# A two-layer recurrent trunk: the keys and values of layer 2 transposed in 32x32 blocks by VectorE and rearranged through DRAM instead of by TensorE, and queries and gates through one Silu

## The chip, the cores and the metric

One core of a Trainium2 chip runs the whole kernel in one launch. The metric is the time on the device in microseconds (us), the median of three runs. The profile shows one more execution, recorded by the hardware profiler. Its engines are TensorE (PE; its loads of the stationary operand are listed as PEld), VectorE (DVE), ScalarE (ACT), GpSimd (POOL) and SyncE (SP), whose queue issues nearly all of the DMAs.

## The reference

One inference step of two layers, for 1024 prompt tokens and 8 samples of 4 tokens each, width 1024. Layer 1 is a gated linear recurrence with a short convolution (RG-LRU). Layer 2, where most of the change lies, is HGRN2: eight heads with 128 key and 128 value channels, a matrix state per head, and an output gate.

```python
def _hgrn_layer(x, g_norm, w_in, lb, o_gain, w_out, S0):
    xn = _rmsnorm(x, g_norm)
    u = (xn @ w_in).astype(jnp.float32)
    q, f, iv, gate = jnp.split(u, 4, axis=-1)
    q = jax.nn.silu(q).reshape(Bsz, T, H_B, DK_B)
    log_g = jnp.logaddexp(jnp.log(lbh), jnp.log1p(-lbh) + jax.nn.log_sigmoid(f.reshape(Bsz, T, H_B, DK_B)))
    k = -jnp.expm1(log_g)
    v = iv.reshape(Bsz, T, H_B, DV_B)
    o, S_T = _hgrn2_chunked(q, k, v, log_g, S0)
    o = o * lax.rsqrt(jnp.mean(o * o, axis=-1, keepdims=True) + EPS) * o_gain.reshape(H_B, DV_B)
    y = (o.reshape(Bsz, T, INNER_B) * jax.nn.silu(gate)).astype(x.dtype)
    return x + y @ w_out, S_T
```

`_hgrn2_chunked` computes, chunk by chunk, causal attention within the chunk under the decays, plus the queries times the state that earlier chunks left; and it carries the state on by the sum over the chunk's tokens of key times value. For that sum the tokens must lie on the contracted axis.

## The kernel before, in words

All activations are kept transposed: 128 channels on the partitions, 1056 tokens (1024 of the prompt, 32 of the samples) along the row. Products are made in single-pass float32 from split operands: x = xh + xl and w = wh + wl, three matmuls a 128x128 block (`mm3`, lines 243 to 245). In layer 1 and for layer 2's first two heads a product has 352 tokens at a time; from the third head on a seven-product scheme (`seven`) makes two projections of a head together from products of 264 tokens.

**The order of the work.** Every operation is entered into a `Flow` with an engine, an estimated cost, the keys that it reads and writes, and a priority. `Flow.plan` lists the operations by a model of the engines, eight times over with due times from a backward pass, and the best list is emitted as it is: each engine then executes its own list in order. In layer 2 the PE operations are chained (`pe`, `main=True`), so PE keeps the order in which the program enters them; what the planner chooses is the order on DVE, ACT, POOL and SP. DMAs go on SP's queue and an instruction there that waits holds up those behind it.

**A head in layer 2.** The projections of a head give queries (row `arow`), the forget gate, from which decays `Gs` and keys (`brow`) are made, output gate (`SG[h]`) and values (`VT`). Between the projection's products of the next heads stand four bursts of small work for the attention:

- `burst1(h)`: decay levels 0 and 1 of head h; keys and values of head h-1 turned so that tokens lie on the partitions (`keys_`, `values`).
- `burst2(h)`: levels 2 and 4 of head h; `states(h-1)`: eight matmuls of `kt` (stationary) with `vt` (moving), one for each chunk of 128 tokens, and the running state in `SA`; the samples' states (`advance`).
- `burst3(h)`: `outs(h-1)`: attention times `vt` plus queries times state, squares and norms into `on`; levels 8 and 16 of head h.
- `burst4(h)`: `gated(h-1)` turns `on` back by PE and multiplies it by the gate; levels 32 and 64 of head h, and the first half of head h's values turned (`values(h, (0,))`).

The last multiply of a head's keys before they are turned is the one of level 64, in `scale` (line 1036), entered in `burst4`. The turning itself is `transposed` (lines 1154 to 1169): four transposes of 128x128 on PE into one PSUM bank, copied by ACT into `kt` or `vt`; it is used four times a head, twice for each of the two. `kt` and `on` are one buffer. `vt` lies in `rows[5]`.

Silu is made of Tanh: z times (1 + tanh(z/2)), twice the Silu. ACT takes the Tanh, DVE multiplies (`scalar_tensor_tensor`), in `first1` (lines 716 and 717) for the first head's queries, in `item` (1009 and 1018) for the rest of heads 0 and 1, and in `settle` (1517 and 1518) from head 2 on. The factor 2 of the queries is made good by 4 times EPS in the norm, that of the gate by `hog`, half the output gain.

Products go into three PSUM banks in turn (`mm`), small work into five (`hg`), while `seven` runs; DVE adds the products together (`plus`, line 1503). Weights come by DMA into five buffers in turn, are added and subtracted by DVE (line 1440), cast by ACT (line 1430), and their rest is taken by POOL (line 325).

## Time and profile before

| | |
|---|---|
| median of 3 runs | 1060.99 us (1060.94 to 1062.35) |
| span of the profiled execution, first to last instruction | 1059.4 us |
| TensorE clock granted, mean | 0.996 |
| layer 1 ends, layer 2 begins, about | 508 us |
| DMA traffic | 103.07 MB, mean 97 GB/s |

The span is that of another execution than the three runs, and it leaves out what lies ahead of the first instruction and behind the last. Busy times are sums over an engine's instructions. Those of PE's matmuls overlap, since they are pipelined: what one costs is seen in the distance from its start to the next one's.

The rows that the next part quotes are of these kinds. A wait: who waited, for whom, us in all, how often, longest. A group of instructions: line, engine, operation, out<-in by the program's names, shapes and count, then busy us and mean ns, then idle us ahead of it. One line's instructions: durations as min/median/max in ns, start of the first and the last. A timeline row: start in us, us that the row covers, and how many instructions are merged in it. A DMA row: count, KB of each, median us from issue to landing.

### The profile page before, as it was taken

The numbers are of one execution on the slowest core, as the hardware profiler recorded it, in microseconds if no ns is written. First come the engines' busy times: TensorE is split into PE (matmuls) and PEld (weight loads), VectorE is DVE, ScalarE is ACT, GpSimd is POOL, SyncE is SP. The second block draws the span as 40 slices with busy tenths as digits, with TensorE's granted clock in tenths as the row PEclk, the third lists the DMA queues.
The fourth block names the chain that finished last, engine by engine and source line by source line (L and its number), as shares of the span: only waits on it lengthen the run. The fifth ranks groups of instructions, "written<-read, shape, count | busy, mean of one in ns | idle before, by whom it ended". The sixth has DMA issues, their size and how long they took to land.

```text
span 1059.4 us, 25677 instructions
## 1 busy us (share of the span) xinstructions
PE 1050.1 (99%) x9964; PEld 1021.2 (96%) x9964; DVE 842.2 (79%) x1671; ACT 590.9 (56%) x1339; POOL 540.0 (51%) x601
## 2 busy tenths in 40 slices
PE   9999999999999999999999999999999999999997
PEld 9999999999999999999999999999999999999986
DVE  7999996888888689265799988988979797994536
ACT  6568656877775875233354474646464555652324
POOL 3425343444544366555667555555545565551544
PEclk9999999999999999999999999999999999999998
DMA  8201112123842595340211121212121221355204
GB/s 297 68 27 45 54 51 74 57 60 100 255 145 63 177 294 162 127 136 28 71 44 38 45 101 44 92 45 92 35 91 54 72 70 66 117 177 167 84 3 164
DMA packets 70121, 103.07 MB, mean 97 GB/s; under 512 B 9200, under 2 KB 50160, under 8 KB 70000
## 3 DMA queue, kind: packets, MB, share of 16 engines
q1 hardware_dynamic: 67696, 98.67, 29.2%
q10 hardware_dynamic: 2304, 2.77, 0.8%
q8 instruction: 78, 1.28, 0.5%
q14 instruction: 43, 0.35, 0.1%
HBM read 71.05 MB, written 25.49 MB: 91 GB/s over the span
## 4 chain that ended last, share of the span: by engine, by line
PE 89%; DVE 6%; DMA 2%; POOL 1%; issue 1%; ACT 0%; ACTq 0%; POOLq 0%; DVEq 0%; SPq 0%
PE mm L243 24%; PE mm L244 24%; PE mm L245 24%; PE hg L569 1%; PE hg L1054 1%; PE hg L1163 1%; DVE R L1370 1%; PE hg L1273 1%; DMA wraw<-in_w_dram 1%; PE hg L1219 1%; PE hg L243 1%; PE hg L244 1%; PE hg L245 1%; PE hg L1275 1%; DVE tmp L1370 1%
## 5 line engine op out<-in xcount | busy, mean ns | idle before, releaser
L243 PE MATMUL mm<-xh,whi 128*128 128x352 f32 (+1 forms) x1143 | 358.6, 314 | 0.0
L245 PE MATMUL mm<-xh,wlo 128*128 128x352 f32 (+1 forms) x1143 | 353.2, 309 | 0.0
L244 PE MATMUL mm<-xl,whi 128*128 128x352 f32 (+1 forms) x1143 | 353.1, 309 | 0.0
L325 POOL TENSOR_TENSOR wlo<-wraw,whi 128x256 fp32r<-128x256 f32 (+3 forms) x184 | 203.3, 1122 | 178.6 <-ACT whi L380 81.2
L244 PEld LDWEIGHTS mm<-xl,whi 128*128 128x128 f32 x1143 | 215.1, 188 | 1.5
L243 PEld LDWEIGHTS mm<-xh,whi 128*128 128x128 f32 x1143 | 214.7, 188 | 1.5
L245 PEld LDWEIGHTS mm<-xh,wlo 128*128 128x128 f32 x1143 | 214.8, 188 | 0.0
L501 DVE SCALAR_TENSOR_TENSOR k<-xb,prm_sb,k 128x352 f32<-128x352 f32 (+2 forms) x144 | 90.1, 637 | 10.9 <-ACT k L498 7.7
L243 PE MATMUL mm<-t,whi 128*128 128x264 f32 (+1 forms) x306 | 89.3, 292 | 0.0
L244 PE MATMUL mm<-t,whi 128*128 128x264 f32 (+1 forms) x306 | 87.7, 287 | 0.0
L245 PE MATMUL mm<-t,wlo 128*128 128x264 f32 (+1 forms) x306 | 87.4, 286 | 0.0
L1503 DVE TENSOR_TENSOR k<-mm,k 128x264 f32<-128x264 f32 x144 | 60.2, 426 | 20.5 <-PE mm L245 17.4
L325 POOL TENSOR_TENSOR wlo<-R,whi 128x256 fp32r<-128x256 f32 x64 | 60.1, 959 | 24.7 <-ACT whi L1430 24.7
L584 POOL TENSOR_TENSOR k<-X 128x352 f32<-128x352 f32 x36 | 44.9, 1257 | 47.8 <-DVE R L585 38.6
L380 ACT CAST whi<-wraw 128x512 fp32r<-128x512 f32 (+2 forms) x83 | 46.1, 574 | 30.1 <-PE mm L244 16.1
L243 PEld LDWEIGHTS mm<-t,whi 128*128 128x128 f32 x306 | 57.6, 188 | 0.2
L245 PEld LDWEIGHTS mm<-t,wlo 128*128 128x128 f32 x306 | 57.7, 188 | 0.0
L244 PEld LDWEIGHTS mm<-t,whi 128*128 128x128 f32 x306 | 57.6, 188 | 0.0
L1430 ACT CAST whi<-wraw 128x512 fp32r<-128x512 f32 x52 | 32.1, 618 | 36.3 <-PE mm L245 16.8
L243 PE MATMUL mm<-yh,whi 128*128 128x352 f32 x153 | 49.9, 326 | 0.0
L245 PE MATMUL mm<-yh,wlo 128*128 128x352 f32 x153 | 49.4, 323 | 0.0
L244 PE MATMUL mm<-yl,whi 128*128 128x352 f32 x153 | 49.4, 323 | 0.0
(481 smaller groups left out, 2634.3 us busy)
## 6 DMA issues: line engine op xcount, KB each, us to landing
wraw<-in_w_dram SPq DMA_DIRECT2D x90, 256.0 KB, 2.7
wraw<-in_wo_dram SPq DMA_DIRECT2D x34, 192.0 KB, 2.5
si<-in_s_in_dram SPq DMA_DIRECT2D x8, 512.0 KB, 3.8
out_ss_out_dram<-si SPq DMA_DIRECT2D x8, 512.0 KB, 2.6
R<-in_w_dram SPq DMA_DIRECT2D x15, 256.0 KB, 2.5
sg<-x1b SPq DMA_DIRECT2D x21, 176.0 KB, 2.9
x<-sg SPq DMA_DIRECT2D x21, 176.0 KB, 1.8
R<-td SPq DMA_DIRECT2D x72, 44.0 KB, 2.0
```

The source lines that it names most:

```text
L243: T.matmul(out, wh, xh, start=first, stop=False)
L244: T.matmul(out, wh, xl, start=False, stop=False)
L245: T.matmul(out, wl, xh, start=False, stop=last)
L325: emit = lambda: e.tensor_tensor(b, x, a.bitcast(F32), op=ALU.subtract)
L380: act(m, lambda hi=hi, raw=raw, m=m: S.copy(hi[:, :m], raw[:, :m]), rk, (hk,), prio)
L501: dve(u, lambda src=src, dst=dst, sh=sh, k=k: V.scalar_tensor_tensor(dst, sh(src, k), pc("cw", 12 * k + m), dst, op0=ALU.mult, op1=ALU.add ...
L569: fl.add("PE", 0.62, lambda ps=ps, i=i, c=c: T.matmul(ps[:96, :CH], gs[:, i, :], ST[:96, chunk(c)], start=True, stop=True), (("gs",), *((" ...
L584: pool(CH, lambda x=x, a=a, b=b: G.tensor_tensor(x, a.bitcast(F32), b.bitcast(F32), op=ALU.add), (ak, bk), (xk,), 3)
L1054: T.matmul(ps[32 * j:32 * j + 32, n * w:n * w + w], B[:, o:o + 32], q(slice(o, o + 32)), start=True, stop=True, tile_position=(0, 32 * j))
L1370: dve(n, lambda: V.tensor_tensor(o, a, b, op=op), r, (w,), prio, True)
L1430: act(512, lambda: S.copy(hi, raw), (rk,), (hk,), 2)
L1503: dve(QT, lambda: V.tensor_tensor(o[0], z[0], u[0], op=ALU.add), (z[1], u[1]), (o[1],), 0)
```

## The change

Two things are changed.

*Turning keys and values.* `transposed` goes. `turned` takes its place, entered at the end of `burst4(h)`, once for the values (source `VT`) and once for the keys (source `brow(h, 0)`). One DVE instruction transposes each 32x32 block of a 128x1024 row within itself; a DMA writes the result, 512 KB, to DRAM (two buffers in turn for each of `vt` and `kt`); four DMAs read it back, one for each 32 partitions, 128 KB each in runs of 256 floats, so that blocks land on the partitions of their tokens. `vt` then holds a chunk's 128 value channels as four runs of 32 neighbouring floats; `kt` holds a chunk's 128 key channels eight floats apart, so that one step runs through all of them. The keys of the planner are four for each of the two, one for each 32 partitions, and all four are waited for.

*Silu.* ACT's Silu activation writes queries and gates at once; DVE's multiply goes, `hog` gives way to the output gain, 4 * EPS to EPS. The forget gate keeps its Tanh. Layer 1's own gates keep Tanh and multiply.

```diff
             if i == 0:
                 o, ok = pairs[1][:, 0, q], [("R", 1, 0, c)]
-                act(CH, lambda: S.activation(o, ps[:, :CH], AF.Tanh, scale=0.5), (pk,), ok, 0)
-                dve(CH, lambda: V.scalar_tensor_tensor(o, o, 1.0, ps[:, :CH], op0=ALU.add, op1=ALU.mult), (pk, *ok), ok, 0)
+                act(CH, lambda: S.activation(o, ps[:, :CH], AF.Silu), (pk,), ok, 0)
...
-        kt = fixed("kt", [128, 8, 128], F32, p1)
-        on = kt
+        on = fixed("kt", [128, 8, 128], F32, p1)
+        kflat = on.rearrange("p n d -> p (n d)")
...
-        vt = rows[5][:, :1024].rearrange("p (n d) -> p n d", n=8)
+        vflat = rows[5][:, :1024]
+        vt, kt = vflat.rearrange("p (a n j) -> p n a j", a=4, n=8), kflat.rearrange("p (a j n) -> p n (a j)", a=4, n=8)
+        VK, KK = ([(o, i) for i in range(4)] for o in ("vt", "kt"))
+        turn = {(o, i): nc.dram_tensor(f"{o}_{i}", (128, 1024), F32, kind="Internal").ap() for o in ("vt", "kt") for i in range(2)}
...
-                    dve(CH, lambda: V.scalar_tensor_tensor(o[:, q], t, 1.0, ps, op0=ALU.add, op1=ALU.mult), (pk, tk), k, 0)
+                    act(CH, lambda: S.activation(o[:, q], ps, AF.Silu), (pk,), k, 0)
...
-        def transposed(row, rk, dst, key, parts):
...
-                        T.transpose(ps[:, n * 128:(n + 1) * 128], row[:, a:a + 128], ident)
...
-                act(512, lambda i=i, ps=ps: S.copy(dst[:, 4 * i:4 * i + 4, :].rearrange("p n d -> p (n d)"), ps), (pk,), ((key, i),), 2)
+        def turned(h, row, rk, dst, key, keys):
+
+            d = turn[key, h % 2]
+            blocks = dst.rearrange("p (b n j) -> p b n j" if key == "vt" else "p (b j n) -> p b n j", b=4, n=8)
+            dve(1024, lambda: V.transpose(blocks, row[:, :1024].rearrange("p (n b i) -> p b n i", n=8, b=4)), rk, keys, 3)
+            dma(d, dst, keys, ((key, "d", h % 2),), 3, 512)
+            back = d.rearrange("(a i) (b m) -> b i a m", a=4, b=4)
+            for b in range(4):
+                dma(dst[32 * b:32 * b + 32].rearrange("p (a m) -> p a m", a=4), back[b], ((key, "d", h % 2),), (keys[b],), 3, 128)
...
-                        T.matmul(ps[:, n * 128:(n + 1) * 128], kt[:, 4 * i + n, :], vt[:, 4 * i + n, :], start=True, stop=True)
-
-                pe(0.94, emit, (("kt", i), ("vt", i)), (pk,))
+                        T.matmul(ps[:, n * 128:(n + 1) * 128], kt[:, 4 * i + n], vt[:, 4 * i + n], start=True, stop=True)
+
+                pe(0.94, emit, (*KK, *VK), (pk,))
...
-            run(together([*([gated(h - 1, *s)] if h else []), *([levels3264(h, *s), values(h, (0,))] if h < H else [])]))
+            run(together([*([gated(h - 1, *s)] if h else []), *([levels3264(h, *s)] if h < H else [])]))
+            if h < H:
+                turned(h, VT, [("VT", c) for c in range(4)], vflat, "vt", VK)
+                turned(h, *brow(h, 0), kflat, "kt", KK)
...
-                act(QT, lambda: S.activation(o[:, q], c, AF.Tanh, scale=0.5), (ck,), k, 0)
-                dve(QT, lambda: V.scalar_tensor_tensor(o[:, q], o[:, q], 1.0, c, op0=ALU.add, op1=ALU.mult), (ck, *k), k, 0, own)
+                act(QT, lambda: S.activation(o[:, q], c, AF.Silu), (ck,), k, 0)
```

57 lines of the change are left out of this document (20 added, 37 removed).

## The prediction

> **What bounds the kernel now.** I read the page's first part, the chain that ended last, TensorE's own waits, and then stretches of the span. First the page:
>
> ```profile
> span 1059.4 us, 25677 instructions
> PE 1050.1 (99%) x9964; PEld 1021.2 (96%) x9964; DVE 842.2 (79%) x1671; ACT 590.9 (56%) x1339; POOL 540.0 (51%) x601
> PE 89%; DVE 6%; DMA 2%; POOL 1%; issue 1%; ACT 0%; ACTq 0%; POOLq 0%; DVEq 0%; SPq 0%
> ```
>
> TensorE (PE) is busy for 1050.1 of 1059.4 us and holds 89% of the chain. A busy PE could still hide stalls, so I look at whom it waited for:
>
> ```profile
> PE hg L730 <- DVE ones L255: 1.0, 1, 1.0
> PE hg L1108 <- DVE a L1036: 0.5, 1, 0.5
> PE mm L243 <- DVE sg L529: 0.5, 1, 0.5
> PE mm L1683 <- DVE sg L1673: 0.4, 1, 0.4
> PE hg L1054 <- DVE R L1066: 0.4, 1, 0.4
> ```
>
> All its waits come to 2.8 us. A matmul taken from this stream is therefore worth its slot, as long as nothing else becomes late. What could become late shows in the stretches (length, then busy us of PE, PEld, DVE, ACT and POOL, the granted clock, DMA share, GB/s):
>
> ```profile
> 568.00:616.00 48.00, 48.00 (x642) 46.26 (x639) 46.46 (x103) 22.90 (x66) 29.29 (x32) 1.00 0.14 47
> 729.00:786.00 57.00, 57.00 (x819) 55.12 (x820) 47.92 (x105) 30.96 (x80) 31.99 (x38) 1.00 0.20 68
> ```
>
> One steady head takes 57 us with VectorE (DVE) at 47.9, 84%. Where layer 2 starts, DVE fills 46.5 of 48 us. PE binds everywhere, DVE almost does at the start, ACT, POOL and the DMA engines do not.
>
> **The change, part by part.**
>
> *The removed transposes.* Per head `transposed` issues sixteen 128x128 transposes, in four blocks of four. PE's timeline of one head gives each block's slot as the distance from its start to the next group's:
>
> ```profile
> 743.91 0.28 PE L243 MATMUL mm<-t,whi 128*128 128x264 f32 x1
> ...
> 744.51 0.28 PE L245 MATMUL mm<-t,wlo 128*128 128x264 f32 x1
> ...
> 745.85 0.66 PE L1163 MATMUL hg<-ident,sg 128*128 128x128 f32 x4
> 746.34 0.60 PE L1163 MATMUL mm<-ident,sg 128*128 128x128 f32 x4
> 746.77 0.38 PE L1175 MATMUL hg<-ident,krep 128*96 128x128 f32 x2
> 746.99 0.60 PE L1163 MATMUL hg<-ident,sg 128*128 128x128 f32 x4
> 747.43 0.38 PE L1175 MATMUL hg<-ident,vrep 128*96 128x128 f32 x2
> ...
> 786.18 0.66 PE L1163 MATMUL mm<-ident,sg 128*128 128x128 f32 x4
> 786.60 0.37 PE L243 MATMUL mm<-t,whi 128*128 128x264 f32 x1
> ```
>
> 0.49 + 0.43 + 0.44 + 0.42 = 1.78 us a head (the durations overlap and would count too much; so do those of the products, whose matmuls follow each other at (744.51 - 743.91) / 5 = 0.12 us), and 8 heads x 1.78 = **14.2 us**. The weight loads of line 1163 number 104 + 24 = 128 = 8 x 16, so all heads are in it. The copies from PSUM behind them (line 1169) leave ScalarE (ACT), which is not on the path; I count nothing for them. Four PSUM banks a head fewer are asked for (one in burst 4, three in burst 1); PE never waited for one, so nothing there either.
>
> *What PE keeps but reads differently.* `states` now takes its weights from kt with eight floats, 32 bytes, between neighbours, and `vt` as four runs of 32 floats. The runs are long and I count nothing for them. The weights are the open cost:
>
> ```profile
> L1163 PEld LDWEIGHTS hg<-ident,sg x104: 138/141/146, 550.2 to 967.8; 128*128 128x128 f32 x104
> L1163 PEld LDWEIGHTS mm<-ident,sg x24: 137/140/146, 568.0 to 966.8; 128*128 128x128 f32 x24
> L1219 PEld LDWEIGHTS hg<-sg,kt x96: 186/192/192, 583.8 to 978.6; 128*128 128x128 f32 x96
> L1054 PEld LDWEIGHTS hg<-R,sg x704: 106/109/113, 534.6 to 871.0; 128*32 128x32 f32 x176
> ```
>
> ```profile
> 757.77 1.16 PE L1219 MATMUL hg<-sg,kt 128*128 128x128 f32 x8
> 758.77 1.06 PE L1219 MATMUL mm<-sg,kt 128*128 128x128 f32 x8
> 759.75 0.64 PE L1227 MATMUL hg<-si,ab 128*32 128x128 f32 x16
> ```
>
> A load of 32 columns takes 109 ns and one of 128 takes 192: 83 ns for 96 columns, 0.86 ns a column, and some 82 ns fixed. The 128 columns alone, 110 ns, fill the slot that a load and its matmul have (0.98 us / 8 = 122 ns) nearly to the end, so a slower load shows at once. Contiguous columns are no proof for strided ones, so the bounds are: nothing, if a column at 32 bytes still comes in 0.86 ns; and, from the fastest reading that the trace has, the transposes' loads with (141 - 82) / 128 = 0.46 ns a column. Those pass 16 bytes in 1.84 ns. If a strided column cost as much as 16 contiguous bytes, a load would need 236 ns, 236 - 122 = 114 ns beyond its slot, and 128 loads (16 a head, as the two rows of eight show) 14.6 us: the whole gain. Which row is nearest? The load of line 1219 itself, same data type, same 128 columns, and it runs at half the column rate that the transposes' loads reach, so there is room for a slower read. I take **nothing**, and keep 14.6 us for the range.
>
> [...]
>
> *VectorE.* What goes, and the nearest rows for what comes:
>
> ```profile
> L1518 DVE SCALAR_TENSOR_TENSOR sg<-sg,k 128x264 f32<-128x264 f32 x24 | 13.8, 595 | 0.0
> L1518 DVE SCALAR_TENSOR_TENSOR R<-R,k 128x264 f32<-128x264 f32 x24 | 13.4, 562 | 0.2 <-ACT R L1517 0.2
> ...
> L1066 DVE TENSOR_TENSOR R<-R,ST 128x1056 f32<-128x1056 f32 x8 | 12.2, 1523 | 4.0 <-POOL ST L722 3.7
> ```
>
> ```profile
> L1018 DVE SCALAR_TENSOR_TENSOR sg<-k,mm x6: 505/510/522, 517.2 to 592.6; 128x352 f32<-128x352 f32 x6
> L1018 DVE SCALAR_TENSOR_TENSOR R<-k,mm x3: 506/507/521, 542.0 to 551.6; 128x352 f32<-128x352 f32 x3
> ```
>
> Silu takes the multiply away: 13.8 + 13.4 + 9 x 0.51 = 31.8 us, and a little more at the end of layer 1 (line 717, and the one small operation for `hog`), which I leave out. The activation that stays has the same shape, so I give Silu Tanh's time. Two block transposes of 128x1024 a head come, sixteen in all. By line 1066 one takes 1.523 x 1024 / 1056 = 1.48 us. Below, 0.74, if one source goes twice as fast as two; above, 3.0, if the strided write of kt costs double. Taken: 16 x 1.48 = 23.7 us, so DVE loses 8; ends -20 (16 x 0.74) and +4 (8 x 1.48 + 8 x 3.0). At 84% that is covered. In the start-up stretch it is about even: nine multiplies, 4.6 us, against 3.0 us for head 0's two transposes and the same for head 1's; if it is not covered, PE waits there for what DVE has over, a few us once. The transpose into kt also waits until PE has turned the outputs that lie there (line 1317), but the level-64 multiply that it needs comes later anyway.
>
> *The way through DRAM.* A head adds two writes of 512 KB and eight reads of 128 KB on SP's queue, each read behind its write's landing:
>
> ```profile
> si<-in_s_in_dram SPq DMA_DIRECT2D x8, 512.0 KB, 3.8
> out_ss_out_dram<-si SPq DMA_DIRECT2D x8, 512.0 KB, 2.6
> wraw<-in_wo_dram SPq DMA_DIRECT2D x7, 128.0 KB, 2.2
> ```
>
> kt's source is ready when the level-64 multiply of the keys ends. In the steady head and in the last one that was:
>
> ```profile
> 735.34 0.69 DVE L1036 TENSOR_TENSOR sg<-sg 128x512 f32<-128x512 f32 x1
> ...
> 956.62 0.69 DVE L1036 TENSOR_TENSOR sg<-sg 128x512 f32<-128x512 f32 x1 [0.85 <-ACT attn L1122]
> ```
>
> ```profile
> 978.06 0.89 PE hg L1219 x8
> ```
>
> Two transposes (3.0), a write (2.6) and four reads (2.2 to 3.8) make 7.8 to 9.4 us, say 11 with hops and issue. `states` starts at 757.77, 22 us after 735.34, and in the last head at 978.06, 21 us after 956.62 (by the chain's row). PE loses 1.4 us of transposes in between, so 8 us of slack stay: hidden. Traffic grows by 16 x 1 MB; the DMA engines are 20% busy in a steady head. New waits: SP stands at the first read until its write has landed, some 2.6 us, and behind it stand weight loads, which ACT, POOL and at last PE want. They wait for a free buffer far longer as it is:
>
> ```profile
> SPq L312 <- POOL wlo L325: 221.6, 91, 19.4
> ```
>
> `states` now waits for all eight reads instead of ACT's copies; behind it stands everything on PE, which is why the slack counts.
>
> *The sum.* Span 1059.4 - 14.2 = 1045.2. The median of the runs, 1060.99, lies 1.6 above the span, so 1046.8; I forecast **1047**.
>
> **The rivals.**
>
> *A, strided weights at up to a line's rate.* For: the load fills its slot, each element lies on its own 16 bytes. Against: the load runs at half the rate of the transposes' loads. Price 4 to 14.6 us, beyond what the forecast's own range allows: 1051 to 1061.
>
> *B, strided weights beyond it (the slower side).* Same place: from 111 ns extra a load (14.2 / 128), that is 233 ns of columns or 1.82 ns a column, the change loses. At 2.2 ns a column, 282 - 122 = 160 ns x 128 = 20 us: 1067. For: nothing shows that scattered reads reach the rate of contiguous ones; against: the same row as in A.
>
> *C, the transposes hold DVE.* A product takes 1.45 us (12 matmuls at 0.12), three banks hold products, so an add may come some 2.9 us late. A transpose and the add behind it,
>
> ```profile
> 736.06 0.43 DVE L1503 TENSOR_TENSOR k<-mm,k 128x264 f32<-128x264 f32 x1
> ```
>
> stall PE in each head by what the transpose lasts beyond 2.5 us. At 4.3 us it eats the gain (8 x 1.8); at 3.0, only 4 us: 1051. For: DVE 97% full at the start; against: 31.8 us leave DVE.
>
> *D, the data come late.* A blocked SP or a crowded queue in the last heads uses up the 8 us of slack, above all where the loads of the output projection crowd. Each late head costs what is missing, 1 to 3 us: 1048 for one head, 1071 for eight.
>
> *E, table loads.* If Silu and Tanh can't be resident together, each head switches twice (queries, forget gate, queries) at
>
> ```profile
> L588 ACT ACT_TABLE_LOAD x12 | 15.4, 1283 | 0.2
> ```
>
> 2.6 us of ACT in a head where it idles 26; PE would see at most a fraction, 0 to 1 us a head: 1047 to 1055. [...]
>
> That the transposes stay on PE in another form can't be: the new text has none.
>
> **How the numbers follow.** Forecast 0.40 (1045 to 1050); A 0.22; B 0.16; C 0.11; D 0.07; E 0.04. This kernel's measurement can tell 0.2%, 2.1 us, from no change: faster is below 1058.9, slower above 1063.1. Faster: 0.40 + A 0.13 + C 0.03 + D 0.03 + E 0.04 = 0.63. Same: A 0.09, C 0.02, D 0.01 = 0.12. Slower: B 0.16, C 0.06, D 0.03 = 0.25. The range begins at 1044 (slots a fifth larger) and ends at 1067, B's 2.2 ns; left out are B beyond that (0.10) and the upper ends of C and D (0.08).
>
> **What would show it.** Right: no line 1163 on PE; loads of `states` still 192 ns and eight in about 0.98 us; PE's waits in all still a few us; DVE busy less than 842. A or B: these loads above 192 ns, eight in 1 to 2.3 us. C: PE waiting for the adds behind a transpose. D: PE waiting at `states` for a DMA into kt or vt. E: table loads inside the heads. Wrong altogether if PE's busy time outside `states` grows.

## The result, and the profile after

The changed kernel takes 1074.12 us (median of 4 runs, 1071.57 to 1075.56), the kernel before 1061.13 us (1060.94 to 1062.35) beside it: a ratio of 1.0119, 95% interval 1.0104 to 1.0135. Run a second time it was 1073.31 to 1060.97 us, 1.0116 (1.0101 to 1.0131). I had forecast 1047 us with a range that ended at 1067: the sign is wrong, and the time lies beyond the range.

The head of the page of the changed kernel:

```profile
span 1073.4 us, 25462 instructions
PE 1059.2 (99%) x9836; PEld 1030.5 (96%) x9836; DVE 836.7 (78%) x1626; ACT 574.6 (54%) x1308; POOL 514.9 (48%) x601
```

PE issues 128 instructions fewer, as forecast, and VectorE is 5.5 us less busy; yet PE is busy for 9 us longer. The transposes (line 1163 before) are gone, so some other work of PE has grown. The loads of kt, by their line (count: minimum/median/maximum in ns, first and last start):

```profile
L1207 PEld LDWEIGHTS hg<-sg,kt x120: 312/335/338, 588.9 to 993.7; 128*128 128x128 f32 x120
L1207 PE MATMUL hg<-sg,kt x120: 401/402/507, 588.9 to 993.8; 128*128 128x128 f32 x120
```

Their median was 192 ns and is 335. What that does to the path stands in the chain that ended last, in the last head:

```profile
990.45 1.86 PE mm L1207 x8
992.31 1.90 PE hg L1207 x8
```

Eight products take 1.86 and 1.90 us; the chain of before had 0.89 for eight, and the timeline 0.98. That is the sign that the prediction gave for rivals A and B. The time from one product's start to the next start on PE, summed over all 128 in the two traces, went from 15.7 to 31.8 us, 16.1 us more, while the transposes' slots in the trace of before made 14.15 us: 2 us on balance, of a difference of 14.0 between the spans. So strided weights are a part of it and not the whole.

For the rest I need marks that stand in every kernel: the first diagonal products of layer 2 (line 1054 before), the first 264-token product (that is where head 2's seven products begin), and the first product with `xh` as its second operand, in the last projection. Each row has the first start after the colon and the three durations. The kernel before:

```profile
L1054 PE MATMUL hg<-R,a x768: 196/218/243, 521.1 to 870.5; 128*32 128x64 f32 x96, 128*32 128x32 f32 x96
L243 PE MATMUL mm<-t,whi x306: 280/285/391, 599.3 to 1010.0; 128*128 128x264 f32 x144, 128*128 128x352 f32 x9
L243 PE MATMUL mm<-t,xh x36: 274/297/398, 1010.5 to 1043.1; 128*128 128x512 f32 x12, 128*128 128x288 f32 x12, 128*128 128x256 f32 x12
```

The changed kernel (line 1055 is 1054 of before):

```profile
L1055 PE MATMUL hg<-R,a x960: 196/219/243, 524.2 to 938.4; 128*32 128x64 f32 x103, 128*32 128x32 f32 x89
L243 PE MATMUL mm<-t,whi x306: 281/285/393, 607.5 to 1024.5; 128*128 128x264 f32 x144, 128*128 128x352 f32 x9
L243 PE MATMUL mm<-t,xh x36: 274/296/398, 1025.0 to 1057.5; 128*128 128x512 f32 x12, 128*128 128x288 f32 x12, 128*128 128x256 f32 x12
```

It is 3.1 us late where layer 2 begins (524.2 against 521.1), though of the change only the first head's three activations and one small operation lie ahead of that; it loses another 5.1 us until head 2 (607.5 - 524.2 = 83.3 against 78.2) and 6.3 us from there to the last projection (417.5 against 411.2). What PE waited for, and the stretches where layer 2 begins (length, busy us of PE, PEld, DVE, ACT and POOL, granted clock, DMA share, GB/s):

```profile
PE hg L1055 <- DVE sg L1037: 2.0, 1, 2.0
PE hg L1207 <- DMA kt<-kt: 1.2, 1, 1.2
PE hg L1109 <- DVE attns L1062: 1.1, 1, 1.1
```

```profile
538.00:543.00 5.00, 4.61 (x86) 4.28 (x71) 4.90 (x8) 2.52 (x8) 3.73 (x4) 1.00 0.02 3
543.00:548.00 5.00, 2.25 (x131) 2.14 (x132) 5.00 (x6) 1.56 (x3) 2.21 (x2) 0.79 0.35 108
548.00:553.00 5.00, 5.00 (x20) 5.00 (x19) 4.90 (x12) 1.24 (x2) 0.00 (x0) 0.53 0.50 164
```

PE waits twice for VectorE (the first and the third row), which is full (4.90, 5.00 and 4.90 of 5 us), and behind the two waits the granted clock falls to 0.79 and 0.53: (1 - 0.79) x 5 + (1 - 0.53) x 5 = 3.4 us that no wait shows. These are means; within them the clock stands at half for 6.8 us without a break, from 545.9 on. Matmuls of 352 tokens then follow each other every 293 ns instead of 161, so a little under half of such a stretch is lost (3.1 us of the 6.8); where half is counted below, it is an upper bound:

```profile
549.00:552.00 3.00, 3.00 (x12) 3.00 (x11) 2.93 (x8) 0.49 (x1) 0.00 (x0) 0.50 0.43 141
```

Behind the second row, a wait for kt's data in head 1, it is at half for another 3.4 us, which is up to 1.7 us lost. In the kernel before, the clock was 1.00 all through the stretch where layer 2 begins. Of VectorE's own new instructions one is smaller and one larger than the 1.48 us that I took for both:

```profile
L1159 DVE STREAM_TRANSPOSE kt<-sg 128x1024 f32<-128x1024 f32 x8 | 18.1, 2266 | 0.1
L1159 DVE STREAM_TRANSPOSE sg<-sg 128x1024 f32<-128x1024 f32 x8 | 9.9, 1240 | 13.1 <-PE hg L1261 13.1
```

They take 1.24 us written in runs of 32 elements and 2.27 us written with 32 bytes from element to element; the sixteen come to 28.0 us, where I took 23.7.

**Theories.** S: the strided weights cost 16 us. Beside it, for the other 10 to 12 us: O, the planner. A list of steps that differs by a few draws another order of DVE's, ACT's, POOL's and SP's instructions, in layer 1 too (its list is improved by a random search with a fixed seed), and the new order is worse than the planner's model of the engines says. F: the function, Silu itself. V: VectorE has no room for the transposes where layer 2 begins. D: the data come late through DRAM.

### The profile page after: what moved, and what is told of

It is laid out like the page before. It is cut to its first block, busy times and chain, and to the rows that moved or that the text cites. A ratio compares the mean times of both kernels' runs of the same rounds, so it can differ in the third digit from the quotient of the medians.

```text
span 1073.4 us, 25462 instructions
## 1 busy us (share of the span) xinstructions
PE 1059.2 (99%) x9836; PEld 1030.5 (96%) x9836; DVE 836.7 (78%) x1626; ACT 574.6 (54%) x1308; POOL 514.9 (48%) x601
## 5 line engine op out<-in xcount | busy, mean ns | idle before, releaser
L325 POOL TENSOR_TENSOR wlo<-wraw,whi 128x256 fp32r<-128x256 f32 (+3 forms) x184 | 191.5, 1056 | 202.9 <-ACT whi L380 105.7
L501 DVE SCALAR_TENSOR_TENSOR k<-xb,prm_sb,k 128x352 f32<-128x352 f32 (+2 forms) x144 | 89.2, 629 | 14.8 <-ACT k L498 11.6
L325 POOL TENSOR_TENSOR wlo<-R,whi 128x256 fp32r<-128x256 f32 x64 | 55.2, 884 | 28.0 <-ACT whi L1421 28.0
```

The costliest lines, as they stand in the source:

```text
L325: emit = lambda: e.tensor_tensor(b, x, a.bitcast(F32), op=ALU.subtract)
L501: dve(u, lambda src=src, dst=dst, sh=sh, k=k: V.scalar_tensor_tensor(dst, sh(src, k), pc("cw", 12 * k + m), dst, op0=ALU.mult, op1=ALU.add ...
```

## The experiments

The times stand beside those of the kernel before on the same chip. Of each edit the lines that decide are shown; the rest of it follows from them and is left out. The three marks of each kernel are read from its own rows of the lines shown above:

| kernel | median, us | before, us | ratio, 95% interval | layer 2 begins | head 2 begins | last projection |
|---|---|---|---|---|---|---|
| before (profile) | | | | 521.1 | 599.3 | 1010.5 |
| e1 changed kernel | 1073.31 | 1060.97 | 1.0101 to 1.0131 | 524.7 | 606.7 | 1022.3 |
| e2 strided kt alone | 1077.29 | 1060.97 | 1.0138 to 1.0168 | 521.1 | 601.2 | 1026.7 |
| e3 Silu alone | 1072.55 | 1060.97 | 1.0090 to 1.0123 | 524.7 | 607.5 | 1022.2 |
| e4 change, plain kt | 1056.34 | 1060.97 | 0.9950 to 0.9972 | 525.6 | 604.2 | 1005.9 |
| e5 Silu, before's order | 1060.31 | 1060.78 | 0.9986 to 1.0005 | 521.0 | 598.8 | 1009.8 |
| e6 turn alone | 1074.97 | 1060.78 | 1.0123 to 1.0156 | 521.1 | 602.3 | 1024.3 |
| e7 turn, plain kt, Tanh | 1062.15 | 1060.78 | 0.9999 to 1.0023 | 520.6 | 600.8 | 1010.3 |
| e8 the same with Silu | 1060.94 | 1060.78 | 0.9992 to 1.0021 | 521.2 | 601.0 | 1011.8 |
| e9 e4, layer 1 in before's order | 1053.49 | 1061.19 | 0.9915 to 0.9945 | 521.2 | 600.6 | 1002.1 |
| e10 heads 2 to 7 turned | 1056.91 | 1061.19 | 0.9947 to 0.9976 | 521.3 | 603.3 | 1006.1 |
| e11 heads 0 and 1 turned | 1066.19 | 1061.19 | 1.0035 to 1.0069 | 520.9 | 601.8 | 1014.4 |
| e12 three strides (one run) | 1068.67 | 1061.19 | | 521.0 | 600.0 | 1017.9 |
| e13 change, plain kt, before's order | 1066.65 | 1060.97 | 1.0030 to 1.0059 | 522.3 | 599.7 | 1013.8 |
| e14 change, before's order | 1072.84 | 1060.97 | 1.0094 to 1.0124 | 520.9 | 602.5 | 1021.2 |
| e15 before in e3's order | 1076.82 | 1060.97 | 1.0132 to 1.0163 | 525.3 | 607.6 | 1027.1 |
| e16 one empty step | 1060.95 | 1060.97 | 0.9992 to 1.0010 | 522.2 | 600.1 | 1011.3 |
| e17 e13, copy later | 1058.76 | 1061.16 | 0.9966 to 0.9993 | 521.2 | 598.8 | 1007.6 |
| e18 heads 0 to 5 so | 1052.98 | 1060.76 | 0.9910 to 0.9944 | 521.1 | 598.6 | 1001.8 |

From the last projection's first product to the end every one of them takes 48.4 to 49.3 us, so the three marks hold nearly the whole difference.

### e1: the changed kernel again

No edit.

> The changed kernel again, beside the kernel before on one chip, for two things. Theory S (strided weights): the 16 us that its 128 products of kt and vt take beyond before's are the cause, the transposes' 14 us are indeed gone, and the rest is a stall at the start of layer 2. Then the products run at about 235 ns each again and the whole comes out 12 to 14 us over the kernel before. Theory L (the chip of the first run): layer 1, in which neither kernel differs but for two activations, was 2.7 us later in the changed kernel's profile; if that was the chip, it is within 1 us here and the difference is 10 to 12 us.

12.3 us over the kernel before. Layer 2 begins at 524.7, 3.6 us late, and in e2 on the same chip at 521.1: theory L falls, the delay in layer 1 belongs to the kernel. Until head 2 it loses 3.8 us more (82.0 against 78.2) and then 4.4 (415.6 against 411.2).

### e2: the strided weights alone

```diff
-        kt = fixed("kt", [128, 8, 128], F32, p1)
-        on = kt
+        on = fixed("kt", [128, 8, 128], F32, p1)
+        kt = on.rearrange("p n d -> p (n d)").rearrange("p (d n) -> p n d", n=8)
...
-S.copy(dst[:, 4 * i:4 * i + 4, :].rearrange("p n d -> p (n d)"), ps)
+S.copy(dst[:, 4 * i:4 * i + 4, :], ps.rearrange("p (n d) -> p n d", n=4))
```

> The kernel before, its transposes on TensorE and its Tanh with multiply kept; only kt is laid out as the changed kernel has it (column after column, eight chunks side by side, 32 bytes from one element of a stationary operand to the next), which ScalarE's copy writes. Theory S: weight loads of kt 312 to 338 ns as in the changed kernel, eight products 1.88 us in place of 0.98, and 15 to 18 us more than before (1076 to 1079). Rival M (a moving operand in runs of 128 bytes is what is slow, that is vt, which is plain here): loads 192 ns, within 2 us of before.

16.3 us more than before. The loads, as a group of the costliest-groups view (busy us, mean ns, idle before):

```profile
L1219 PEld LDWEIGHTS hg<-sg,kt 128*128 128x128 f32 x96 | 23.5, 334 | 0.2
L1219 PEld LDWEIGHTS mm<-sg,kt 128*128 128x128 f32 x32 | 8.0, 334 | 0.1
```

The same 334 ns with `vt` as plain as before, so M falls and S stands. Nothing else moved much: layer 2 begins at 521.1 as before, 1.9 us are lost by head 2 (head 0's products) and 14.3 from there on (seven heads, 2.0 each).

### e12: three strides at once

```diff
+        k4 = flat[:, :512].rearrange("p (d n) -> p n d", n=4)
+        k2 = flat[:, 512:768].rearrange("p (d n) -> p n d", n=2)
+        k1 = flat[:, 768:].rearrange("p (n d) -> p n d", n=2)
```

> The kernel before, kt laid out with 16 bytes from element to element in chunks 0 to 3, 8 bytes in 4 and 5, side by side in 6 and 7; ScalarE's copy writes them so. It tells what the load's price hangs on. If each new line of 16 bytes costs, 8 bytes are dearer than 4 by less than 16 is, and 16 bytes cost what 32 did (312 to 338 ns); if the bytes passed over cost, 16 bytes lie between 192 and 335 ns; if any step over 4 bytes has one price, 8 and 16 both cost 335 ns.

Line 1233 has 16 bytes from element to element, 1235 has 8, 1237 has 4:

```profile
L1233 PEld LDWEIGHTS hg<-sg,kt 128*128 128x128 f32 x48 | 11.6, 326 | 0.2
L1235 PEld LDWEIGHTS hg<-sg,kt 128*128 128x128 f32 x24 | 3.4, 201 | 0.0
L1237 PEld LDWEIGHTS hg<-sg,kt 128*128 128x128 f32 x24 | 3.2, 192 | 0.0
```

16 bytes cost nearly what 32 do (326 and 334 ns), 8 bytes nearly what 4 do (201 and 192). Neither the bytes passed over nor the mere presence of a step sets the price, and it isn't the number of 16-byte pieces that hold the 128 elements in proportion either: from 32 pieces (4 bytes) to 64 (8 bytes) it is 9 ns, from 64 to 128 (16 bytes) it is 125. Of the three guesses the first comes nearest: 8 bytes add less than 16 do (9 ns against 134), and 16 cost about what 32 did. What makes the jump between 8 and 16 bytes isn't shown. The one run took 1068.67 us, 7.5 over before, for half of the products.

### e4: the weights made plain again

```diff
-        kflat = on.rearrange("p n d -> p (n d)")
+        kt = on
+        kflat = SA[:, :1024]
...
+                for i in range(2):
+                    n = slice(4 * i, 4 * i + 4)
+                    act(512, lambda n=n: S.copy(kt[:, n].rearrange("p n (a j) -> p n a j", a=4), kl[:, n]), [*KL, *SK], KK[2 * i:2 * i + 2], 2)
```

`kl` is the view of `kflat` that `vt` is of `vflat`: VectorE writes in runs of 32, and ScalarE makes the weights contiguous.

> The changed kernel with one thing put back: the weights lie side by side. VectorE turns the keys' blocks in runs of 32 into the row of the states (free at that time), they go through DRAM into that row, and ScalarE copies them from there into a plain kt, two copies of 128x512 a head (the kernel before had these copies too). Theory S: loads of kt 192 ns, eight products 0.98 us, 16 us less than the changed kernel: 1056 to 1060, so at or a little below the kernel before; what is left of the transposes' 14 us goes to the start of layer 2 and to data that come later by the copies' 1.5 us. Rival D (late data are the cost, the loads only fill the wait): no faster than the changed kernel, as the copies make the data later still.

17.0 us less than the changed kernel, and 4.6 less than the kernel before. The loads are back:

```profile
L1209 PEld LDWEIGHTS hg<-sg,kt 128*128 128x128 f32 x120 | 14.0, 192 | 2.1 <-ACT sg L1513 1.8
```

The runs of `vt` cost nothing: the 128 slots of load and product make 15.5 us here, 15.7 before. From head 2 to the last projection it takes 401.7 us, 9.5 less than before: the heads do gain. It gives half of it back ahead of head 2, where it is 4.9 us late. D falls as the main cause.

### e3 and e5: Silu alone, in a new order and in before's order

e3 has the change's Silu lines in the kernel before and nothing else. e5 has the same, but an empty step stays in the planner's list for each multiply that goes. In `settle`, e3 and then e5:

```diff
-                act(QT, lambda: S.activation(o[:, q], c, AF.Tanh, scale=0.5), (ck,), k, 0)
-                dve(QT, lambda: V.scalar_tensor_tensor(o[:, q], o[:, q], 1.0, c, op0=ALU.add, op1=ALU.mult), (ck, *k), k, 0, own)
+                act(QT, lambda: S.activation(o[:, q], c, AF.Silu), (ck,), k, 0)
```

```diff
+                act(QT, lambda: S.activation(o[:, q], c, AF.Silu), (ck,), k, 0)
+                dve(QT, lambda: None, (ck, *k), k, 0, own)
```

> The kernel before with only the queries' and output gates' Silu, transposes and plain kt kept. Theory S: DVE is not TensorE's bound, so within 2 us of before. Rival P (the order that the planner finds is what stalls the start of layer 2, and the Silu shifts it): 3 to 6 us slower than before with TensorE waiting for DVE in the 538 to 553 stretch.

> Silu alone cost 11.6 us, and this asks how. Every Silu stands in it and VectorE's multiplies are gone, but the planner is given an empty step where each multiply stood, so that all other instructions keep the order that they have in the kernel before (the queries and gates of heads 0 and 1 issue their Silu where the multiply stood). Theory O (the order): taking steps out of the planner's list made it draw another order for layer 1 and for the start of layer 2, and that order is worse. Then this kernel is within 2 us of before, 1059 to 1062, with TensorE's 2.9 us wait at the first diagonal products of layer 2 gone. Rival F (the function: Silu's own time on ScalarE, its table load, the later ready queries): 1070 to 1073 still, with the wait in its place.

e3 is 11.6 us slower than before, and Theory S had expected nothing; e5 is 0.5 us faster, which is no difference by its interval. The two hold the same work. What PE waits for in e3 (the first two rows) and in e5:

```profile
PE hg L1053 <- DVE sg L1035: 2.9, 1, 2.9
PE mm L243 <- DVE k L1502: 2.5, 2, 2.0
```

```profile
PE hg L730 <- DVE ones L255: 1.0, 1, 1.0
PE mm L1683 <- DVE sg L1673: 0.9, 1, 0.9
PE hg L1054 <- DVE R L1066: 0.6, 1, 0.6
```

In e3 PE stands at the first diagonal products for 2.9 us and the clock falls behind it:

```profile
543.00:548.00 5.00, 1.92 (x130) 1.65 (x129) 4.97 (x9) 2.00 (x4) 1.79 (x3) 0.73 0.18 56
548.00:553.00 5.00, 5.00 (x21) 5.00 (x21) 4.93 (x10) 1.65 (x3) 0.90 (x1) 0.59 0.02 5
```

e5 has none of it, and its layer 2 begins at 521.0. So F falls, and O explains the whole of Silu's 11.6 us: 3.6 in layer 1, 4.6 more until head 2, 3.5 behind that. In layer 1 no wait of PE shows it. Between 100 and 508 us of before's trace e3 falls back by 2.4 us, a few ns at a time and at a clock of 1.00 in both: behind a product of `xl` with the weights `whi`, for one, the next matmul starts after 161.2 ns on average instead of 159.1. Why the other order is slower there isn't shown. Rival E of the prediction falls too: there is one table load for Silu, 1.28 us at the end of layer 1 (at 489.4 us in the changed kernel, 486.6 in e5), and none inside the heads.

### e15: the kernel before in e3's order

```diff
-                act(QT, lambda: S.activation(o[:, q], c, AF.Tanh, scale=0.5), (ck,), k, 0)
-                dve(QT, lambda: V.scalar_tensor_tensor(o[:, q], o[:, q], 1.0, c, op0=ALU.add, op1=ALU.mult), (ck, *k), k, 0, own)
+                act(QT, lambda: (S.activation(o[:, q], c, AF.Tanh, scale=0.5),
+                                 V.scalar_tensor_tensor(o[:, q], o[:, q], 1.0, c, op0=ALU.add, op1=ALU.mult)), (ck,), k, 0)
```

> The kernel before with its Tanh and multiply, nothing of the change in it, but in the order of e3: the planner's list holds one step for both (so it counts nothing for the multiply on VectorE), and both are issued there. Theory O: the 11 us of e3 appear without any Silu, 1069 to 1075, 3.5 us of them in layer 1. Rival F2 (Silu and its order only hurt together): within 2 us of before.

15.9 us slower with no part of the change in it, more than expected:

```profile
PE mm L243 <- DVE k L1502: 4.5, 7, 2.1
PE hg L1053 <- DVE sg L1035: 3.2, 1, 3.2
```

The marks up to head 2 are those of e3 (525.3 and 607.6 against 524.7 and 607.5). Its instructions stand in e3's order on PE and POOL, and on VectorE but for the 60 multiplies; against before, some 820 of VectorE's 1671 stand elsewhere. The 4.3 us beyond e3 come with the multiplies, which the planner doesn't know of here. With e5 this closes the square: both kernels in before's order are at 1060 to 1061 us, both in the other order at 1073 to 1077.

### e16: one empty step

```diff
         own_gate(0)
+        dve(264, lambda: None, (), (), 5)
```

> The kernel before with one empty step added to the planner's list where layer 2 begins, counted as a VectorE addition of 128x264. It moves some 30 of VectorE's instructions and nothing else; layer 1 is as before. It tells how much a small move of the order can cost. Theory O: 1 to 6 us, with a wait at the start of layer 2 and a lower granted clock behind it. If order matters only in large moves: within 1 us.

Nothing (0.02 us), with some 40 of VectorE's instructions in other places. A miss for O in its strong form: not every move of the order costs.

### e6, e7 and e8: the turn without Silu, and with a plain kt

e6 is the changed kernel with Tanh and its multiply put back in all three places; e7 is e4 with these put back; e8 is e7 with Silu and empty steps as in e5. Layer 1 is planned as before in all three. In `settle`, e6 and e7:

```diff
-                act(QT, lambda: S.activation(o[:, q], c, AF.Silu), (ck,), k, 0)
+                act(QT, lambda: S.activation(o[:, q], c, AF.Tanh, scale=0.5), (ck,), k, 0)
+                dve(QT, lambda: V.scalar_tensor_tensor(o[:, q], o[:, q], 1.0, c, op0=ALU.add, op1=ALU.mult), (ck, *k), k, 0, own)
```

> The other half of the change by itself: transposes by VectorE and DRAM with the strided kt, and Tanh with its multiply as before; layer 1 is then planned as before to the instruction. Theory S with O: 14.2 us of transposes go, 16.1 us of strided loads come, layer 2's start keeps some of its stall (its list of steps changes here too): 1061 to 1066, with layer 1 on time at 508 us. Rival F gives the same for the heads, so this tells whether the two halves add up: 11.6 and this difference should sum to the changed kernel's 12.3.

> The turn by VectorE and DRAM with the keys copied into a plain kt by ScalarE, and Tanh with its multiply as before. Theory S with O: this is my prediction's sum without its two faults, 14 us below before: 1046 to 1050; what can be missing is the stall at the start of layer 2. Rival F gives the same. Rival D (the copies make the data late, TensorE waits for them at the products of kt and vt): 1050 to 1058, with a wait for ACT's copy of kt in several heads.

> The same with Silu, the empty steps left in the planner's list. Theory O: 1045 to 1049, as the run with Tanh or a little below it since VectorE has less to do. Rival F: 1056 as the run with Silu and the plain kt.

All three miss. e6 is 14.2 us slower than before, 9 us above the top of what was expected; e7 is 1.4 slower and e8 the same within 0.2, where 11 to 16 us of gain were expected. The halves don't add: 11.6 and 14.2 are not 12.3, since each list draws an order of its own. Layer 2 begins on time in all three, as O says. In e6 PE waits then:

```profile
PE hg L1057 <- DVE sg L1039: 2.5, 1, 2.5
PE hg L1142 <- DVE sg L1039: 2.1, 1, 2.1
PE mm L243 <- DVE k L1496: 1.4, 1, 1.4
```

once in head 0, once in head 1, each with a stretch of low clock behind it:

```profile
543.00:548.00 5.00, 4.88 (x85) 4.87 (x86) 4.97 (x9) 1.79 (x4) 1.02 (x1) 0.75 0.35 131
...
621.00:626.00 5.00, 5.00 (x40) 4.88 (x37) 4.21 (x11) 3.33 (x8) 0.00 (x0) 0.70 0.01 3
```

These are six us of waits. The clock is at half for 3.4 us from 542.1 and again from 620.6 (the first of the two rows cuts this off in part), which costs up to 1.7 us each time, another 3.4 in all. e6 is 12.8 us above e7, where the loads alone make 16.

### e9: layer 1 in before's order

e4 with an empty step behind the Silu of `first1`, and the small operation for `hog` left in layer 1; layer 2 as in e4.

```diff
                 act(CH, lambda: S.activation(o, ps[:, :CH], AF.Silu), (pk,), ok, 0)
+                dve(CH, lambda: None, (pk, *ok), ok, 0)
```

> The run e4 (turn, plain kt, Silu, layer 2 planned with it) with one thing put back: empty steps in the planner's list of layer 1, so that layer 1 has before's order to the instruction; layer 2 is planned as in e4. Theory O: e4 stood 4.2 us behind before at 508 us though nothing of the change runs there; that goes, and 1056.3 becomes 1051 to 1053. Rival R (the drift belongs to the function or the program's size, not to the order): 1055 to 1057, still 3 to 4 us behind at 508 us.

1053.49 us, 7.7 less than before and just above what O expected: the 4.5 us of layer 1 are gone (521.2), so R falls. e8 and e9 hold the same work; only layer 2's list differs, by the empty steps: 1060.94 and 1053.49. That is O again, with 7 us.

### e10 and e11: some heads by VectorE, the others by TensorE

e7 in which a head outside `TURN` has the transposes of the kernel before; e10, and e11 with `TURN = range(HC)`, where HC is 2:

```diff
+        TURN = range(HC, H)
...
-            if h < H:
+            if h in TURN:
                 turned(h, VT,
...
+            yield from together([*([] if h in TURN else [transposed(B, bk, kt, KK, (0, 1))]), samples(krep, "krep", s, sk, 64, kst, "kst", 1)])
```

> As e7 (Tanh, plain kt), but heads 0 and 1, those beside the building of the sums, keep their transposes on TensorE; heads 2 to 7 are turned by VectorE and DRAM. Theory V (VectorE is the bound where layer 2 starts, and 2 to 3.5 us of its transposes a head and another order there cost TensorE 7 to 9 us of waits and clock): no such stall, 1.6 us less for each of six heads, some of it lost in the last one: 1050 to 1054. Rival D (what e7 lacked is lost to late data all along): 1058 to 1062.

> The counterpart: only heads 0 and 1 are turned by VectorE and DRAM, heads 2 to 7 keep TensorE's transposes; Tanh, plain kt. Theory V: the 7 to 9 us of the start stay, less 3 us for two heads' transposes: 1064 to 1069, though the change then takes work off TensorE. Rival D: 1058 to 1061.

1056.91 us, 3 us above the top of what V expected, and 1066.19. In e11 two turned heads cost 5 us instead of gaining 3, as V expected. But in e10 heads 0 and 1 are as before, and still it is 4.0 us late at head 2:

```profile
543.00:548.00 5.00, 4.07 (x78) 4.07 (x79) 4.97 (x10) 1.24 (x2) 1.39 (x2) 0.75 0.29 93
548.00:553.00 5.00, 5.00 (x30) 5.00 (x30) 3.03 (x8) 2.65 (x8) 0.75 (x1) 0.91 0.00 0
```

So V as I had put it falls: most of it isn't the transposes' time on a full VectorE. Each of the new lists so far stalls there, with or without transposes in the stretch, all but e16's.

### e13 and e14: the whole change in before's order

The planner gets before's list. The 32 transposing steps of PE and ScalarE's copies stay in it empty, and VectorE's transpose with its DMAs is issued where the first values' transpose stood, or behind the level-64 multiply of the keys. e13 has a plain kt, copied by ScalarE where the copies out of PSUM stood; e14 has the strided kt. Both have Silu as in e5.

```diff
+                    if level == 64 and not s:
+                        turned(h, brow(h, 0)[0], kflat, "kt")
...
+                pe(0.49, lambda i=i: turned(h, VT, vflat, "vt") if key == "vt" and not i else None, rk, (pk,))
...
+                act(512, lambda i=i: plain(i) if key == "kt" else None, (pk,), ((key, i),), 2)
```

> The change (Silu, both turns through VectorE and DRAM) with a plain kt, in before's order: the planner is given before's list of steps, its 32 transposing steps empty, VectorE's transpose and the DMAs behind it issued where the first values' transpose or the keys' last scaling stood. Theory O (the order alone is what went wrong besides the strides): the transposes' 14 us are gained whole, 1045 to 1049. Theory V (VectorE has no room for the transposes at the start of layer 2): 3 to 8 us of waits there, 1050 to 1056.

> The change as it is, strided kt included, in before's order. Theory O: 14 us off, 16 us on, 1061 to 1064, so 10 to 12 us less than the changed kernel with the same instructions. Theory V: 1066 to 1072.

Both miss: 1066.65 and 1072.84. e14 is only 0.5 us faster than the changed kernel with nearly the same instructions, where O expected 10 to 12. In part O holds: both begin layer 2 nearly on time, and in e13 its start is 0.8 us shorter than before's (599.7 - 522.3 = 77.4 against 78.2), where head 0's transposes should give 1.8; PE waits there once for VectorE, 1.8 us. In e14 that wait is 2.6 us, half clock for 3.4 us stands behind it, and the start is 3.4 us longer than before's, though head 0's strided products (1.9) and its transposes (-1.8) cancel. That is a part of what V expected. And heads 2 to 7 lose what they should gain; in e13 PE waits seven times for VectorE's adds, 6.8 us in all. ScalarE in e13, in head 1 and in the last head (start, us, idle time before and its end in brackets):

```profile
637.50 1.14 ACT L1189 COPY kt<-a 128x512 f32<-128x512 f32 x2 [4.68 <-DMA a<-kt]
638.55 0.25 ACT L1197 CAST kst<-hg 96x128 fp32r<-96x128 f32 x1
...
974.17 1.14 ACT L1189 COPY kt<-a 128x512 f32<-128x512 f32 x2 [8.70 <-DMA a<-kt]
975.22 0.25 ACT L1197 CAST kst<-hg 96x128 fp32r<-96x128 f32 x1
```

In before's order the copy stands early, since transposes on PE were there early. ScalarE works its row in order, so it stands 4.7 and 8.7 us for the data from DRAM, and behind it the samples' copies and all that hangs on them. Before's order was good for before's waits; a change that makes an operand come some 10 us later (in e17's rows below, 9.5 us from the write's issue to the last read's) needs another place for its reader.

### e17: the copy one burst later

```diff
-                act(512, lambda i=i: plain(i) if key == "kt" else None, (pk,), ((key, i),), 2)
+                act(512, lambda: None, (pk,), ((key, i),), 2)
...
+            pe(0.6, lambda: (h and (plain(0), plain(1)), diag(ps[:, :256], B1, lambda q: A1[:, q], 32)), (*a1k, *b1k), (pk,))
```

> e13 with one thing moved: ScalarE's two copies into the plain kt are issued one burst later, just ahead of the products that read them, no longer ahead of the copies of the samples. Theory A (ScalarE, in order, stood at kt's copy until the data came, and the samples, VectorE and TensorE behind it): the waits for VectorE's adds in the heads go, 1.5 us a head are gained as in e4 and e9, and the last heads lose less: 1048 to 1056. Rival Q (SyncE's row and the queue are the cause, its reads that wait for their writes): within 3 us of e13's 1066.7.

1058.76 us, 7.9 less than e13 and just outside what A expected. At 922 us of the profile of before, the same product starts 10.06 us earlier than there, the transposes' gain of six heads nearly whole (6 x 1.78 = 10.7). Then 7 us are lost beside the last projection, for the most part in two waits of PE and the clock, which is at half for 3.4 us behind each:

```profile
PE mm L243 <- DVE k L1525: 2.9, 1, 2.9
PE hg L1241 <- ACT kt L1189: 2.0, 1, 2.0
```

SyncE, ScalarE and VectorE ahead of the first:

```profile
900.08 0.45 SPq L1170 DMA_DIRECT2D kt<-a  x1
907.02 2.51 SPq L1173 DMA_DIRECT2D a<-kt  x4
...
911.00 0.42 SPq L312 DMA_DIRECT2D k<-yd  x1
```

```profile
914.86 0.48 ACT L1611 CAST t<-k 128x352 fp32r<-128x352 f32 x1 [6.77 <-DMA k<-yd]
```

```profile
915.37 0.53 DVE L325 TENSOR_TENSOR t<-k,t 128x352 fp32r<-128x352 f32 x1 [3.37 <-ACT t L1611]
```

SyncE issues kt's write at 900.08 and gets its four reads out between 907.02 and 909.53, once the write has landed. The load of `yd`, which stands behind them, goes at 911.00; ScalarE waits 6.8 us for it, VectorE 3.4 for ScalarE, and PE 2.9 for VectorE's add behind that. The second wait is `states` itself, in the last head: there the copy of kt comes late.

### e18: the last two heads by TensorE again

e17, but heads from `LAST` on have the transposes of the kernel before:

```diff
+        LAST = 6
...
-                    if level == 64 and not s:
+                    if level == 64 and not s and h < LAST:
```

> e17 with the last two heads, 6 and 7, transposed by TensorE as in the kernel before; heads 0 to 5 are turned by VectorE and DRAM, in before's order, with a plain kt and Silu. Theory Q (beside the output projection SyncE's row and the DMA queue have no room for the way through DRAM: its reads stand until their write has landed and the loads of the projection behind them): the 10 us that e17 had gained at 922 us stay, 1049 to 1053, the fastest of all. Rival (the last heads' losses come from an order that does not fit the shorter heads, whatever turns them): 1055 to 1060.

1052.98 us, ratio 0.9927 (0.9910 to 0.9944): Q holds, with both of e17's waits gone. At head 2 it is 0.7 us early, at the last projection 8.7 us, and PE's waits are again few:

```profile
PE hg L1063 <- DVE R L1075: 1.7, 1, 1.7
PE hg L730 <- DVE ones L255: 1.0, 1, 1.0
```

So the turn through DRAM pays 1.45 us a head (8.7 / 6) where three things are given: plain weights, an order that fits, and a queue with room. With e9 it is the fastest version found; both beat both kernels.

## Why the prediction was wrong

**Where the 11.9 us between the spans of e1 and of before went** (1071.3 - 1059.4). Layer 1 is 3.6 us late. Until head 2 come 3.8 more: head 0's strided products, 1.9 in e2, and its transposes, 1.8 less, nearly cancel, and waits and clock where layer 2 begins make some 3.7. From head 2 to the last projection come 4.4. The starts of the same projection products in both traces, just ahead of each group of small work and just behind it, part these: `states` costs 14.8 us more in seven heads, the transposes' places give 11.9 back (0.41 and 1.28 us a head, 1.69 in all, where their slots were 1.78), and 1.5 lie elsewhere, 0.9 of them between 931.5 and 936 us of before's trace, where e1's PE waits 0.6 us for VectorE's rest of a split operand (`xl`, line 325). e9, with plain weights, gains 9.7 there: the same 11.9 less one wait of 2.0 us for a DMA into vt in head 1, and some tenths.

1. *The removed transposes*: forecast 14.2. The 14.15 above is the same sum over before's slots, no measurement of the gain; what a head gains is 1.69 us (e1, e9), 13.5 for eight. Right, to 5%.
2. *What PE keeps but reads differently*: "I take **nothing**" is the step that failed first. The upper bound of that same paragraph, 16 contiguous bytes a column and 114 ns beyond the slot, was close: a product's slot went from 123 to 249 ns, 126 more. That a column should cost what 16 bytes cost, rival A's "line", was an assumption that no run shows; the runs showed loads of 326 ns with 16 bytes from element to element and 334 with 32, beside 192 with 4 and 201 with 8 (e12, e2). The 126 ns are past the 111 ns from which B has the change lose. B was the right rival at 0.16; reckoned its way, the slot measured is 1.95 ns a column (249 / 128), 128 x 126 ns = 16.1 us, and with the sum of the prediction 1063. I chose the lower end because the load "runs at half the column rate that the transposes' loads reach"; that room was not there.
3. *A step that the prediction didn't have*: it counted each edit at the place where it stands and took the rest of the program to stay as it was. The order is computed from the list of steps, so each removed step is an edit of everything. That is worth 3.6 us in e1's layer 1 (e9 shows it by taking it away), the 11.6 us of e3, 7 us between e8 and e9. For the 3.7 us where e1's layer 2 begins the order as cause is argued from e3 and e15, which stall at the same place without the turn; e14, in before's order, loses nearly as much there by another wait. An order is not good in itself: before's suits before's waits. The front of this document tells of the planner; the prediction used it nowhere. No row of before's trace shows another order's time. The hint was there: PE waited 2.8 us in all although VectorE filled 46.5 of 48 us where layer 2 begins, and the same work in another list, e15, does not manage that.
4. *VectorE*: "if it is not covered, PE waits there for what DVE has over, a few us once" came true, at its place, but for the most part not by its working: e10 loses 4.0 us there with no transpose of VectorE in the stretch, e13 only some 1 us with both. Rival C's transposes (2.5 us and more) are not it either: they take 1.24 and 2.27.
5. *The clock*: no term had it. Behind many of the waits of 2 to 3 us the clock is at half for 3.4 or 6.8 us, which costs up to 1.7 or 3.4: 5.1 us in the changed kernel's first profile, 1.7 in e1, 3.4 in e6.
6. *The way through DRAM*, "hidden" with 8 us of slack: right for `states` in the steady heads from head 2 on, as e17's gain up to 922 us shows. In head 1 it was late in some runs: 1.2 us in the changed kernel's first profile (none in e1), 2.0 in e9. In the changed kernel's own order little is lost beside the last projection, so rival D has next to no part in its time. It came true in e17, which loses 7 us there, and e18 wins them back; what was late then were the loads behind the waiting reads, and once `states`. From the end of the write's row at 900.53 to the first read at 907.02 SyncE stood 6.5 us there, where the prediction took 2.6.
7. *Silu at Tanh's time, no table loads in the heads*: right; the activations of 128x264 take a median of 430 and 425 ns as Silu (e5), 431 and 425 as Tanh. VectorE is 24.0 us less busy in e5 (842.2 - 818.2), not 31.8: the means of 595 and 562 ns hold a few long ones, the median of line 1518 is 424. That was worth 0.5 us, within the noise: nothing to PE, as the prediction said.

## What to carry to other kernels

Before taking work off the bounding engine, check in what steps it will read its operands: a stationary operand with 32 bytes from element to element doubled the cost of load and product here (a slot of 249 ns instead of 123), which was more than the transposes that it saved. Where a program plans its own order from a list, try each edit first with empty steps left in the list: that parts the price of the edit from the price of a new draw, and here the draw alone was worth 12 us between e3 and e5. And in a queue that works in order, an operand that now comes 10 us later (9.5 in e17's rows) needs its reader moved back in the row, and its own requests kept away from loads that others wait for.

## What the runs showed of the hardware

- A load of 128x128 float32 weights took 192 ns with 4 bytes from element to element, 201 with 8, 326 with 16 and 334 with 32 (e12, e2). Behind the slow loads the matmul's duration in the profile, whose end is modelled, grew as well, from a median of 275 ns to 402; the slot of the two went from 123 to 249.
- VectorE's transpose in 32x32 blocks, 128x1024 float32: 1.24 us written in runs of 32 elements, 2.27 with 32 bytes between neighbours.
- Behind a wait the clock granted to TensorE can fall to half. In the traces of these runs it does so for 3.4 or 6.8 us at a time, and matmuls of 352 tokens then follow each other every 293 ns instead of 161. Of the 21 waits of 1.9 to 3.2 us that they hold between 515 and 1000 us, 16 were followed by this within 4 us and five were not, among them one of 3.0 us (e14) and one of 2.0 (e3). In e4 two of 1.5 and 1.6 us close together cost nothing; behind two of 1.7 and 1.6 in e9 the clock was at half for 3.4 us. So the length of a wait alone does not decide it in these runs; what does isn't shown.
- SyncE's queue works in order. In e17 it stood 6.5 us (900.53 to 907.02) at the first read back of kt until the write had landed, and the four reads went out between 907.02 and 909.53; a load behind them went at 911.00, and ScalarE waited 6.8 us for it.
